# Keys and queries as half-precision pairs with a power of two per channel, the exponential undoing the power by its scale

## The chip, the cores and the metric

One Trainium2 chip; the kernel uses one of its cores. A core has TensorE (PE; its weight loader is listed apart as PEld), VectorE (DVE), ScalarE (ACT), GpSimd (POOL) and SyncE (SP), each taking its own instructions in order, and 16 DMA engines fed by queues. The metric is the device time of one execution in microseconds (us). A profiled execution gives a trace of every instruction.

## The reference

A trunk of two layers over 2048 tokens of width 1024: a Mamba-2 mixer, then multi-head latent attention (16 heads), then a final norm. The change touches the attention alone:

```python
ckv, k_rope = split(rms_norm(h, kv_g_in) @ kv_w_down)       # 256 and 32 columns
kv = rms_norm(ckv, kv_g_latent) @ kv_w_up                   # per head: k_nope 64, v 64
k_rope = rope(k_rope)
q  = rms_norm(cq, mla_g_q) @ mla_w_uq                       # per head: q_nope 64, q_rope 32
s  = (q_nope @ k_nope.T + q_rope @ k_rope.T) * 96 ** -0.5   # 96 channels
p  = softmax(where(causal, s, -inf))
o  = p @ v
```

The arithmetic is float32.

## The kernel before

Three stages follow each other: Mamba over four blocks of 512 tokens and four groups (16 items, each a scan of four chunks with the gemms of the next item between its steps), the projections of the attention (`mla`), and the attention itself (`heads`, about 2086 to 3010 us of the trace), then the output projection (`back`).

**A product of float32 accuracy** is three matmuls, `mm3` (lines 85 to 87): high part by high part, high by low, low by high. The parts come from `split` (lines 115, 116; with a scale of one value per channel 118, 119) as float32r pairs, or from `pair16` (lines 123, 124) as float16 pairs; in both ACT makes the high part and DVE the remainder. Already in half precision are most of Mamba's gemms, the values V and the probabilities. Keys and queries are float32r: `mla_up` writes them by `out` (channels without rotation) and `rope`, through POOL's DMA queue into `kn_d`, `qn_d`, `q1_d`, `q2_d`, `kr_d`, and `load_k`, `load_q` bring each head's back as tiles K (96 x 2 x 2048) and Q (96 x 2 x 512).

**The attention.** A head has four query blocks q of 512; each has four rows j of 128 queries, called q.j below. A row's keys up to the diagonal are cut into at most four pieces of 256 to 512 keys (3.1 has 3.1a to 3.1d; 40 pieces a head: 25 of 512 keys, 7 of 384, 8 of 256). The work on a piece and on its row:

- S: on PE, `mm3` of Q and K into one of four PSUM banks; the last piece of a row gets the mask by one more matmul (line 1062).
- M: on DVE, the maximum of the piece (line 1063). N: after the last piece, the row's negated maximum (line 1067).
- E: on ACT, the exponential of a piece, bias N, with its sum (line 1075; an ACTIVATE and a short ACTIVATION_READ_ACCUMULATOR). Only when it has ended is the piece's bank free: S of a piece waits for the E of the piece four before.
- T: a unit of 128 keys by up to four rows of probabilities is transposed on PE (line 1090, up to four transposes); P copies it to float16 on ACT (line 123), Q makes the low half on DVE (line 124), and V on PE multiplies it with the values (lines 1100, 1101). O, r and s are small steps at the end of a block or row.

PE's order here is written by hand: `CREDIT` says which T and V come after each piece, 20 pieces behind the scores. DVE, ACT and POOL take theirs from a scheduler when the program is built; the order is fixed from then on. Units are counted within a head, so T24, P24, Q24, V24 are one unit's steps.

PE's order, the same in every head (from row 2.0 on, cut):

```
S2.0c V10 V11 T15 V12 S2.1a T16 V13 S2.1b S2.1c V14 ... S2.3b S2.3c T24 V20 V21
S3.0a T25 S3.0b S3.0c S3.0d V22 V23 T26 T27 V24 T28 V25
S3.1a T29 S3.1b V26 S3.1c S3.1d V27 T30 T31 V28 T32 V29
S3.2a T33 S3.2b V30 S3.2c V31 S3.2d T34 V32 T35 T36 V33
S3.3a T37 V34 S3.3b V35 S3.3c S3.3d T38 V36 T39 V37 T40   S0.0a V38 T41 S0.1a (next head)
```

Of the kernel before, what the change touches and what calls it, by code (L numbers as in the profile page):

```python
# [9 lines left out]
F32 = mybir.dt.float32  # L10
# [10 lines left out]
P = 128  # L21
# [47 lines left out]
class Net:  # L69
# [205 lines left out]
    def constants(self, cp):  # L275
# [6 lines left out]
        for name, n in PACKED:  # L282
            setattr(self, name, self.pack[:, at:at + n])
            at += n

    def layer_constants(self, cp):
        nc, a = self.nc, self.a
# [41 lines left out]
    def mamba(self, cp):  # L329
# [45 lines left out]
        self.tail = self.outp(*items[-1])  # L375

    def value_scale(self):
# [29 lines left out]
        for k in range(2):  # L407
            nc.gpsimd.dma_start(self.wv_d[k * P:(k + 1) * P, :], raw[k])

    def load_x(self, b, src, tag="hx"):  # L410
# [404 lines left out]

    def rope(self, p1, p2, cos, sin, d1, d2, n, t0):
# [45 lines left out]
    def mla_kv_down(self, b, tables):  # L862
# [10 lines left out]
        for j in range(2):  # L873
# [3 lines left out]
            pk.append(ps)  # L877
        self.rope(pk[0], pk[1], *tables, self.kr_d[0:16], self.kr_d[16:32], 16, b * TB)

# [36 lines left out]
    def mla_up(self, b, tables):  # L916
# [11 lines left out]

        def out(ps, d):
# [15 lines left out]
        while ahead:  # L945
            (n, w), ahead = ahead, next(todo, None)
            qT = self.qT
            for i in range(2 if n == 6 else 4):
                r0 = n % 2 * 512 + i * P
                if n < 2:  # L950
                    out(chan(cT, w, i, "tr"), self.kn_d[r0:r0 + P])
                elif n < 4:
# [8 lines left out]
                elif n < 6:  # L961
                    out(chan(qT, w, i, "mm"), self.qn_d[r0:r0 + P])
                else:
                    self.rope(chan(qT, w, i, "mm"), chan(qT, w, i + 2, "mm"), *tables, self.q1_d[i * P:(i + 1) * P],
                              self.q2_d[i * P:(i + 1) * P], P, t0)
                yield
# [53 lines left out]
    def heads(self, sp):  # L1020
# [15 lines left out]
        def scores(h, qb, st):  # L1036
# [8 lines left out]
            for j in range(4):  # L1045
# [20 lines left out]
                nm = self.t(sp, "nm", [P, 1], bufs=4)  # L1066
                v.tensor_reduce(nm, mx[:, :nb], AX.X, ALU.max, negate=True)  # L1067
                p = {}
# [3 lines left out]
                def exp(n, j=j, nb=nb, parts=parts, banks=banks, nm=nm, p=p, sm=sm):  # L1072
                    s, w = banks[n]
                    x = self.t(sp, "Pr", [P, TB], bufs=NP)
                    nc.scalar.activation(x[:, :w], s[:, :w], AF.Exp, bias=nm, accum_out=sm[:, n:n + 1])  # L1075
                    for c in range(0, w, P):
# [195 lines left out]
    def run(self):  # L1272
        tc = self.tc
        with ExitStack() as whole:
# [8 lines left out]
            self.ri_d = dp.tile([NH, T], F32, name="ri_d")  # L1283
            self.qn_d = dp.tile([1024, 2, T], F32, name="qn_d")
            self.q1_d = dp.tile([256, 2, T], F32, name="q1_d")
            self.q2_d = dp.tile([256, 2, T], F32, name="q2_d")
            self.kn_d = dp.tile([1024, 2, T], F32, name="kn_d")
            self.kr_d = dp.tile([32, 2, T], F32, name="kr_d")
            self.v_d = dp.tile([T, 2048], F16, name="v_d")
# [60 lines left out]
```

## Time and profile before

| | us |
|---|---|
| median of 3 runs (3198.4 to 3201.17) | 3201.06 |
| the profiled execution | 3198.45 |
| its span, first to last instruction | 3196.7 |

The profile gives instructions with their line, engine, operation and tile (`mm<-K,xT` is a PSUM tile written from K and a Q tile, whose buffer is named xT), their start and duration, and the idle time of the engine before one with what ended it. Durations of neighbours overlap, since an engine starts an instruction before the one ahead has drained: what an instruction costs in a stream is the distance of two starts, what it costs in a chain is its duration. The start of a first matmul behind a weight load is modelled early; the starts of the second and third are not. A row "x4" in order of time merges equal neighbours: its duration reaches from the first start to the last end.

### The profile page before, as it was taken

How to read it: one execution, taken by the hardware profiler on the slowest of the kernel's cores; microseconds unless marked ns; L12 is line 12 of the kernel's file. 1: busy time of each engine (PE TensorE's matmuls, PEld its weight loads, DVE VectorE, ACT ScalarE, POOL GpSimd, SP SyncE). 2: the span in 40 equal slices, each digit the busy share in tenths (PEclk: the TensorE clock that was granted, in tenths of full speed). 3: DMA queues.
4: the chain of work that ended last, by engine and by line, in shares of the span. 5: the costliest groups of instructions: out<-in, count | busy, mean ns of one | idle time of the engine just before them, and what ended most of it. 6: DMA issues, size and time to landing. Idle time of an engine off the chain costs nothing.

```text
span 3196.7 us, 51296 instructions
## 1 busy us (share of the span) xinstructions
PE 3098.7 (97%) x17735; PEld 2244.6 (70%) x17735; DVE 2371.4 (74%) x4786; ACT 2016.2 (63%) x5027; POOL 658.8 (21%) x927
## 2 busy tenths in 40 slices
PE   8999999999999999999999999999999999999998
PEld 6787654556655566665878888877777777777777
DVE  6888787777666666766766665678888888888675
ACT  7888576665555464555646554477877778778522
POOL 1222232321122211312111211322222122222100
PEclk9999999999999999999999999999999999999999
DMA  5443656554343345534486655843434434444494
GB/s 176 131 128 125 225 190 230 189 183 154 133 166 125 120 143 185 172 120 138 128 273 222 222 191 192 266 111 77 92 79 85 86 77 92 81 97 104 99 274 158
DMA packets 213236, 482.52 MB, mean 151 GB/s; under 512 B 28976, under 2 KB 62768, under 8 KB 211536
## 3 DMA queue, kind: packets, MB, share of 16 engines
q1 hardware_dynamic: 160672, 316.02, 31.2%
q0 software_dynamic: 52304, 163.22, 18.9%
q8 instruction: 140, 2.29, 0.3%
q14 instruction: 120, 0.98, 0.1%
HBM read 347.02 MB, written 132.12 MB: 150 GB/s over the span
## 4 chain that ended last, share of the span: by engine, by line
PE 65%; DVE 8%; ACT 6%; DMA 5%; issue 2%; POOL 1%; SPq 0%; ACTq 0%; DVEq 0%; POOLq 0%
PE mm L85 13%; PE mm L86 12%; PE mm L87 12%; PE tr L1090 6%; PE tr L1100 3%; PE tr L1101 3%; PE tr L86 3%; PE tr L87 3%; PE tr L85 3%; DVE cacc L495 2%; DMA wraw<-in_ssm_w_in_dram 2%; PE tr L699 1%; ACT Pr L1075 1%; DMA os<-ri_d 1%; DMA big<-cumT 1%
## 5 line engine op out<-in xcount | busy, mean ns | idle before, releaser
L124 DVE SCALAR_TENSOR_TENSOR PTs<-tr,PTs 128x512 f16<-128x512 f32 (+3 forms) x640 | 375.0, 607 | 92.4 <-ACT PTs L123 86.6
L123 ACT ACTIVATE PTs<-tr 128x512 f16<-128x512 f32 (+3 forms) x640 | 328.5, 541 | 141.1 <-PE tr L1090 140.7
L1063 DVE TENSOR_REDUCE mx<-mm 128x1 f32<-128x512 f32 (+2 forms) x631 | 375.7, 608 | 46.8 <-PE mm L87 44.3
L1075 ACT ACTIVATE Pr<-mm,nm 128x512 f32<-128x512 f32 (+2 forms) x631 | 395.7, 636 | 23.1 <-DVE nm L1067 21.4
L1090 PE MATMUL tr<-pack,Pr 128*128 128x128 f32 x2176 | 317.6, 273 | 1.4 <-ACT Os L1107 1.3
L85 PE MATMUL mm<-xT,wsp 128*128 128x512 f16 (+1 forms) x800 | 310.3, 388 | 0.0
L85 PE MATMUL mm<-K,xT 96*128 96x512 f32 (+2 forms) x639 | 287.0, 449 | 23.3 <-ACT Pr L1075 21.9
L86 PE MATMUL mm<-xT,wsp 128*128 128x512 f16 (+1 forms) x800 | 307.6, 384 | 0.0
L87 PE MATMUL mm<-xT,wsp 128*128 128x512 f16 (+1 forms) x800 | 307.3, 385 | 0.2 <-DVE wsp L116 0.2
L1090 PEld LDWEIGHTS tr<-pack,Pr 128*128 128x128 f32 x2176 | 253.2, 141 | 49.8 <-ACT Os L1107 2.1
L495 DVE SCALAR_TENSOR_TENSOR cacc<-craw,pack,cacc 128x512 f32<-128x512 f32 x288 | 219.9, 785 | 27.6 <-ACT cacc L493 25.5
L85 PE MATMUL mm<-wsp,xT 128*128 128x512 f16 (+2 forms) x640 | 235.9, 369 | 3.1 <-ACT craw L489 3.0
L86 PE MATMUL mm<-wsp,xT 128*128 128x512 f16 (+2 forms) x640 | 234.2, 366 | 0.0
L87 PE MATMUL mm<-wsp,xT 128*128 128x512 f16 (+2 forms) x640 | 233.6, 366 | 0.0
L86 PE MATMUL mm<-K,xT 96*128 96x512 f32 (+2 forms) x639 | 231.8, 363 | 0.0
L87 PE MATMUL mm<-K,xT 96*128 96x512 f32 (+2 forms) x639 | 231.2, 362 | 0.0
L1100 PE MATMUL tr<-PTs,xT 128*128 128x512 f16 (+3 forms) x640 | 222.2, 349 | 0.1
L1101 PE MATMUL tr<-PTs,xT 128*128 128x512 f16 (+3 forms) x640 | 219.7, 347 | 0.0
L85 PE MATMUL mm<-wsp,yT 128*128 128x512 f32 x512 | 208.9, 408 | 8.4 <-DMA wsp<-wo_d 4.5
L692 ACT ACTIVATE Xw<-tr,d_wend 128x64 f32<-128x64 f32 x512 | 112.0, 329 | 155.8 <-DVE y L689 127.6
L86 PE MATMUL mm<-wsp,yT 128*128 128x512 f32 x512 | 204.1, 399 | 0.0
L87 PE MATMUL mm<-wsp,yT 128*128 128x512 f32 x512 | 203.9, 398 | 0.0
(421 smaller groups left out, 7417.9 us busy)
## 6 DMA issues: line engine op xcount, KB each, us to landing
wsp<-wo_d SPq DMA_DIRECT2D x96, 512.0 KB, 3.6
wraw<-in_ssm_w_in_dram SPq DMA_DIRECT2D x128, 256.0 KB, 3.0
big<-cumT SPq DMA_DIRECT2D x64, 512.0 KB, 4.7
wsp<-w_d SPq DMA_DIRECT2D x64, 512.0 KB, 3.7
wo_d<-wsp POOLq DMA_DIRECT2D x32, 512.0 KB, 4.6
w_d<-wsp POOLq DMA_DIRECT2D x32, 512.0 KB, 5.0
xT<-qn_d POOLq DMA_DIRECT2D x64, 256.0 KB, 4.6
K<-kn_d POOLq DMA_DIRECT2D x15, 1024.0 KB, 8.4
```

What stands on the lines that cost most here:

```text
L85: mm(out, l_hi, r_hi, start=start, stop=False)
L86: mm(out, l_hi, r_lo, start=False, stop=False)
L87: mm(out, l_lo, r_hi, start=False, stop=stop)
L123: self.nc.scalar.activation(hi, src, AF.Copy, scale=scale)
L124: self.nc.vector.scalar_tensor_tensor(lo, src, scale, hi, ALU.mult, ALU.subtract)
L495: nc.vector.scalar_tensor_tensor(acc, raw[:, k:k + TB], wk[k], acc, ALU.mult, ALU.add)
L692: act(Xw[:, hc], px[:, hc], AF.Copy, scale=wend[:, h0 + h:h0 + h + 1])
L1063: v.tensor_reduce(mx[:, n:n + 1], s[:, :w], AX.X, ALU.max)
L1075: nc.scalar.activation(x[:, :w], s[:, :w], AF.Exp, bias=nm, accum_out=sm[:, n:n + 1])
L1090: nc.tensor.transpose(pt[:, j * P:(j + 1) * P], st["P"][j][kb], self.ident)
L1100: nc.tensor.matmul(st["O"][:, c], vals[h][:, kb, :], u[:, 0], start=kb == 0, stop=False)
L1101: nc.tensor.matmul(st["O"][:, c], vals[h][:, kb, :], u[:, 1], start=False, stop=kb == nk - 1)
```

## The change

Keys and queries become float16 pairs. So that they fit float16, each channel is multiplied by a power of two; the product of the powers of a key channel and its query channel is the same number for all 96 channels of a head, and its inverse is given to the exponential as scale. In parts:

- New `qk_scale`, in the scan of Mamba's item (block 2, group 0), counted as 8 steps beside the item's 32. It bounds each channel by the sum of the weights' absolute values: 14 loads through the three buffers `wraw` (13 of 256 KB), 14 ACT instructions, 52 matmuls with 128 weight columns and 2 moving columns, 16 with 16 weight columns, 3 small ones, and about 25 DVE instructions on at most 24 columns. It fills `aK`, `bQ`, `aR`, `bR`, `sc`, `nsc`.
- In `mla_up` and `rope` the 88 pairs are made by `pair16` with a scale of one value per channel in place of `split` without one. Stores, DRAM tensors and loads have half the bytes; their number stays.
- A float32r matmul loads its weights itself; a float16 one has its own LDWEIGHTS instruction ahead of it (1920 more PE instructions). The wait for the bank is on the matmul, not on the load.
- N is one instruction that joins two maxima and multiplies by `nsc`, and rows of three or four pieces get one more ahead of it (t, 128 in all).
- E has two operands of one value per partition, bias and scale, where it had the bias alone.

PE's order in the attention is unchanged. The built program's orders on ACT and DVE are not; where they matter:

```
ACT  before  P13 P14 P15 E2.0a E2.0b P16 E2.0c
     after   P13 P14 P15 E2.0a P16 E2.0b E2.0c
DVE  before  Q13 Q14 M2.0b M2.0c N2.0 Q15 M2.1a
     after   M2.0b Q13 Q14 M2.0c t Q15 N2.0 M2.1a
DVE  before  M2.3b M2.3c s N2.3 Q24 M3.0a M3.0b s Q25 M3.0c M3.0d Q26 Q27 N3.0 Q28
     after   M2.3b M2.3c s Q24 t N2.3 M3.0a M3.0b M3.0c s Q25 M3.0d t N3.0 Q26 Q27 Q28
ACT  before  P24 E2.3a E2.3b E2.3c P25 O P26 P27 P28 E3.0a E3.0b E3.0c E3.0d P29 P30 P31 E3.1a
     after   P24 E2.3a E2.3b E2.3c P25 O P26 P27 E3.0a P28 E3.0b P29 E3.0c E3.0d P30 P31 E3.1a
ACT  before  E3.1d O P34 E3.2a P35 P36 E3.2b P37 E3.2c E3.2d P38 E3.3a P39 E3.3b P40 E3.3c
     after   E3.1d O P34 P35 P36 E3.2a E3.2b E3.2c P37 E3.2d P38 E3.3a P39 P40 E3.3b E3.3c
```

In Mamba the last chunk of the item's scan now stands among the small matmuls of `qk_scale`: between the item's last gemm and the next item's first, 16, 24, 6, 6 and 16 of them lie between the chunk's own matmuls.

```diff
+            elif g == 0 and b == NB - 2:
+                parts.append(self.qk_scale())
+                total += 8
...
+    def qk_scale(self):
...
+        for u in range(5):
+            ks = 2 if u < 2 else 3
+            src, gain = (a["kv_w_up"], self.gkl) if u < 2 else (a["mla_w_uq"], self.gqs)
+            c0 = u * TB if u < 2 else (u - 2) * TB
+            w = []
+            for k in range(ks):
+                raw = self.t(self.wp, "wraw", [P, TB], bufs=WRAW)
+                nc.sync.dma_start(raw, src[k * P:(k + 1) * P, c0:c0 + TB])
+                if k % 2 == 0:
+                    m = self.t(self.wp, "wsp", [P, 2, TB], F32R, bufs=WSP)
+                nc.scalar.activation(m[:, k % 2], raw, AF.Abs, scale=gain[:, k:k + 1])
+                w.append(m[:, k % 2])
+            yield
+            ps = self.t(self.pp, "tr", [P, TB], bufs=4)
+            for c in range(4):
+                for k in range(ks):
+                    nc.tensor.matmul(ps[:, 2 * c:2 * c + 2], w[k][:, c * P:(c + 1) * P], self.ones_r[:, 0:2],
+                                     start=k == 0, stop=k == ks - 1)
...
-            u = self.ev()
-            self.split(u[:n, 0, :], u[:n, 1, :], x[:n])
-            nc.gpsimd.dma_start(d[:, :, t0:t0 + TB], u[:n].bitcast(F32))
+            u = self.ev(F16)
+            self.pair16(u[:n, 0, :], u[:n, 1, :], x[:n], scale[:n])
+            nc.gpsimd.dma_start(d[:, :, t0:t0 + TB], u[:n])
...
-            u = self.ev()
-            self.split(u[:, 0, :], u[:, 1, :], ps)
-            nc.gpsimd.dma_start(d[:, :, t0:t0 + TB], u.bitcast(F32))
+            u = self.ev(F16)
+            self.pair16(u[:, 0, :], u[:, 1, :], ps, scale)
+            nc.gpsimd.dma_start(d[:, :, t0:t0 + TB], u)
...
-            self.keys[h] = self.t(self.hp, "K", [96, 2, T], F32R, bufs=2)
+            self.keys[h] = self.t(self.hp, "K", [96, 2, T], F16, bufs=2)
...
-        Q = self.quer[h, n] = self.t(self.xq, "xT", [96, 2, TB], F32R, bufs=8)
+        Q = self.quer[h, n] = self.t(self.xq, "xT", [96, 2, TB], F16, bufs=8)
...
-                v.tensor_reduce(nm, mx[:, :nb], AX.X, ALU.max, negate=True)
+                if nb == 1:
+                    v.tensor_scalar(nm, mx[:, 0:1], self.nsc, None, ALU.mult)
+                else:
+                    if nb > 2:
+                        v.tensor_tensor(mx[:, 0:nb - 2], mx[:, 0:nb - 2], mx[:, 2:nb], ALU.max)
+                    v.scalar_tensor_tensor(nm, mx[:, 0:1], mx[:, 1:2], self.nsc, ALU.max, ALU.mult)
...
-                    nc.scalar.activation(x[:, :w], s[:, :w], AF.Exp, bias=nm, accum_out=sm[:, n:n + 1])
+                    nc.scalar.activation(x[:, :w], s[:, :w], AF.Exp, bias=nm, scale=self.sc, accum_out=sm[:, n:n + 1])
```

More of the change, by code (lines that the diff above doesn't have):

```diff
@@ L408, in value_scale @@
             nc.gpsimd.dma_start(self.wv_d[k * P:(k + 1) * P, :], raw[k])
+    def qk_scale(self):
+        nc, v, a = self.nc, self.nc.vector, self.a
+        S = self.t(self.sm, "qkS", [P, 24], bufs=1)
+        v.memset(S, 1.0)
+        for u in range(5):
[16 more added lines that the diff above has]
+                                     start=k == 0, stop=k == ks - 1)
+            v.tensor_copy(S[:, 4 * u:4 * u + 4], ps[:, 0:8].rearrange("p (c n) -> p c n", n=2)[:, :, 0])
+        raw = self.t(self.wp, "wraw", [P, KD, 32], bufs=WRAW)
+        nc.sync.dma_start(raw, a["kv_w_down"][:, 256:288].rearrange("(k p) c -> p k c", p=P))
+        v.tensor_tensor(raw, raw, self.gk.unsqueeze(2).to_broadcast([P, KD, 32]), ALU.mult)
+        m = self.t(self.wp, "wsp", [P, KD, 32], F32R, bufs=WSP)
+        nc.scalar.activation(m, raw, AF.Abs)
+        yield
+        ps = self.t(self.pp, "tr", [P, TB], bufs=4)
+        for k in range(KD):
+            for i in range(2):
+                nc.tensor.matmul(ps[0:16, 0:2], m[:, k, 16 * i:16 * i + 16], self.ones_r[:, 0:2],
+                                 start=k + i == 0, stop=k + i == KD)
+        v.tensor_copy(S[0:16, 20:21], ps[0:16, 0:1])
+        sel = self.t(self.sp, "cacc", [16, P], bufs=2)
+        v.tensor_copy(sel.rearrange("p (n i) -> p n i", n=8), self.ident[0:16, 0:16].unsqueeze(1).to_broadcast([16, 8, 16]))
+        ps = self.t(self.pp, "tr", [P, TB], bufs=4)
+        nc.tensor.matmul(ps[:, 0:1], sel, S[0:16, 20:21], start=True, stop=True)
+        v.tensor_copy(S[:, 20:21], ps[:, 0:1])
+        v.tensor_tensor(S[:, 16:18], S[:, 16:18], S[:, 18:20], ALU.add)
+        v.tensor_scalar(S, S, TINY, None, ALU.max)
+        ei = self.t(self.sm, "qke", [P, 24], I32, bufs=1)
+        v.tensor_scalar(ei, S.bitcast(I32), 23, None, ALU.logical_shift_right)
+        e = self.t(self.sm, "qkf", [P, 24], bufs=1)
+        v.tensor_copy(e, ei)
+        t = self.t(self.sm, "qkt", [P, 16], bufs=1)
+        v.tensor_tensor(t[:, 0:8], e[:, 0:8], e[:, 8:16], ALU.add)
+        v.tensor_scalar(t[:, 8:10], e[:, 16:18], e[:, 20:21], 1.0, ALU.add, ALU.add)
+        v.tensor_reduce(t[:, 10:11], t[:, 0:10], AX.X, ALU.max)
+        yield
+        ps = self.t(self.pp, "tr", [P, TB], bufs=4)
+        nc.tensor.transpose(ps[0:1, 0:P], t[:, 10:11], self.ident)
+        v.tensor_reduce(t[0:1, 11:12], ps[0:1, 0:P], AX.X, ALU.max)
+        ps = self.t(self.pp, "tr", [P, TB], bufs=4)
+        nc.tensor.matmul(ps[:, 0:1], self.ones[0:1, :], t[0:1, 11:12], start=True, stop=True)
+        v.tensor_scalar(t[:, 12:13], ps[:, 0:1], 193.0, None, ALU.max)
+        x = self.t(self.sm, "qkx", [P, 20], bufs=1)
+        v.tensor_scalar(x[:, 0:8], e[:, 0:8], -1.0, 264.0, ALU.mult, ALU.add)
+        v.tensor_scalar(x[:, 8:16], e[:, 0:8], t[:, 12:13], 263.0, ALU.subtract, ALU.add)
+        v.tensor_scalar(x[:, 16:17], e[:, 20:21], -1.0, 263.0, ALU.mult, ALU.add)
+        v.tensor_scalar(x[:, 17:18], e[:, 20:21], t[:, 12:13], 264.0, ALU.subtract, ALU.add)
+        v.tensor_scalar(x[:, 18:19], t[:, 12:13], -146.0, None, ALU.add)
+        v.tensor_scalar(x[:, 0:19], x[:, 0:19], 1.0, 254.0, ALU.max, ALU.min)
+        xi = self.t(self.sm, "qki", [P, 20], I32, bufs=1)
+        v.tensor_copy(xi[:, 0:19], x[:, 0:19])
+        v.tensor_scalar(xi[:, 0:19], xi[:, 0:19], 23, None, ALU.logical_shift_left)
+        f = xi.bitcast(F32)
+        v.tensor_copy(self.aK, f[:, 0:8])
+        v.tensor_copy(self.bQ, f[:, 8:16])
+        v.tensor_copy(self.aR, f[:, 16:17])
+        v.tensor_copy(self.bR, f[:, 17:18].to_broadcast([P, 2]))
+        v.tensor_copy(self.sc, f[:, 18:19])
+        v.tensor_scalar(self.nsc, f[:, 18:19], -1.0, None, ALU.mult)
+        yield
@@ L814, in rope_tables, with rope @@
         return cos, ang
-    def rope(self, p1, p2, cos, sin, d1, d2, n, t0):
+    def rope(self, p1, p2, cos, sin, d1, d2, n, t0, scale):
         nc, v = self.nc, self.nc.vector
@@ L927, in chan, with out @@
             return ps
-        def out(ps, d):
-            u = self.ev()
-            self.split(u[:, 0, :], u[:, 1, :], ps)
-            nc.gpsimd.dma_start(d[:, :, t0:t0 + TB], u.bitcast(F32))
+        def out(ps, d, scale):
+            u = self.ev(F16)
+            self.pair16(u[:, 0, :], u[:, 1, :], ps, scale)
+            nc.gpsimd.dma_start(d[:, :, t0:t0 + TB], u)
         def groups():
@@ L950, in mla_up @@
                 if n < 2:
-                    out(chan(cT, w, i, "tr"), self.kn_d[r0:r0 + P])
+                    out(chan(cT, w, i, "tr"), self.kn_d[r0:r0 + P], self.aK[:, 4 * n + i:4 * n + i + 1])
                 elif n < 4:
@@ L961, in mla_up @@
                 elif n < 6:
[L962 removed]
+                    c = 4 * (n - 4) + i
+                    out(chan(qT, w, i, "mm"), self.qn_d[r0:r0 + P], self.bQ[:, c:c + 1])
                 else:
                     self.rope(chan(qT, w, i, "mm"), chan(qT, w, i + 2, "mm"), *tables, self.q1_d[i * P:(i + 1) * P],
[L965 removed]
+                              self.q2_d[i * P:(i + 1) * P], P, t0, self.bR[:, i:i + 1])
                 yield
```

15 lines of the change are left out of this document (9 added, 6 removed).

## The prediction

> **What bounds the kernel now.** I read the page's head and its busy times first, then the busy times of three windows (the columns are the window, its length, then the busy time and instructions of PE, PEld, DVE, ACT and POOL, the granted clock, the DMA share and GB/s).
>
> ```profile
> span 3196.7 us, 51296 instructions
> PE 3098.7 (97%) x17735; PEld 2244.6 (70%) x17735; DVE 2371.4 (74%) x4786; ACT 2016.2 (63%) x5027; POOL 658.8 (21%) x927
> ...
> 840.00:945.00 105.00, 104.63 (x601) 63.17 (x601) 67.02 (x121) 53.78 (x135) 20.22 (x27) 1.00 0.46 161
> 1800.00:2000.00 200.00, 197.83 (x1027) 170.48 (x1026) 122.09 (x242) 104.63 (x203) 33.73 (x55) 1.00 0.61 201
> 2086.00:3010.00 924.00, 899.27 (x5655) 687.53 (x5654) 772.07 (x1831) 733.72 (x2010) 201.55 (x295) 1.00 0.41 84
> ```
>
> PE sets the pace in all three: the scan where `qk_scale` goes (840 to 945), the projections whose pairs change (1800 to 2000) and the attention (2086 to 3010). In the attention ACT (733.72 of 924) and DVE (772.07) are not far behind; that window alone has matmuls to save. What holds PE up there is told by the group of the first score matmul on the page, and by the view of who waits for the exponential.
>
> ```profile
> L85 PE MATMUL mm<-K,xT 96*128 96x512 f32 (+2 forms) x639 | 287.0, 449 | 23.3 <-ACT Pr L1075 21.9
> ...
>   PEld mm L85: 57.3, 118
>   PE mm L85: 21.9, 21
> ```
>
> PE loses only some 23 us, all at S, all to E: the bank comes free late. Both sides of the change meet here: shorter S, and a longer E that comes at another place of ACT's order.
>
> **Faster score matmuls.** The spacing of starts is the price. Here are a float32r S of 256 keys, one of 384, and a stretch that holds float16 V of 384 columns, then an S of 512.
>
> ```profile
> 2496.33 0.28 PE L86 MATMUL mm<-K,xT 96*128 96x256 f32 x1
> 2496.45 0.28 PE L87 MATMUL mm<-K,xT 96*128 96x256 f32 x1
> ...
> 2521.41 0.34 PE L86 MATMUL mm<-K,xT 96*128 96x384 f32 x1
> 2521.59 0.34 PE L87 MATMUL mm<-K,xT 96*128 96x384 f32 x1
> ...
> 2517.60 0.33 PE L1100 MATMUL tr<-PTs,xT 128*128 128x384 f16 x1
> 2517.77 0.33 PE L1101 MATMUL tr<-PTs,xT 128*128 128x384 f16 x1
> ...
> 2518.49 0.39 PE L86 MATMUL mm<-K,xT 96*128 96x512 f32 x1
> ```
>
> And the stretch in which S3.1a waits today:
>
> ```profile
> 2509.01 1.04 PE L1090 MATMUL tr<-pack,Pr 128*128 128x128 f32 x8
> ...
> 2510.33 0.60 PE L1090 MATMUL tr<-pack,Pr 128*128 128x128 f32 x4
> 2510.76 0.38 PE L1100 MATMUL tr<-PTs,xT 128*128 128x512 f16 x1
> 2510.98 0.38 PE L1101 MATMUL tr<-PTs,xT 128*128 128x512 f16 x1
> 2512.57 0.50 PE L85 MATMUL mm<-K,xT 96*128 96x512 f32 x1 [1.21 <-ACT Pr L1075]
> 2512.90 0.39 PE L86 MATMUL mm<-K,xT 96*128 96x512 f32 x1
> 2513.13 0.40 PE L87 MATMUL mm<-K,xT 96*128 96x512 f32 x1
> ```
>
> A float32r matmul of 512 costs .23 (2512.90 to 2513.13; .233 over several), a float16 one .216 (2510.76 to 2510.98); at 384 it is .18 against .17 (.163 by columns), at 256 .12 against .11. For three matmuls that is .05, .05 and .03 saved. A head has 25, 7 and 8 such pieces: 25 x .05 + 7 x .05 + 8 x .03 = 1.84 us, and 16 heads give **-29 us**, if no wait eats it. The 1920 separate weight loads cost nothing as long as a matmul of .11 or more covers them.
>
> **The longer exponential.** No row has an ACTIVATE with a scale and a bias of one value per partition. The nearest are pairs of groups with none and with one such operand, first from SBUF, then from PSUM:
>
> ```profile
> L115 ACT ACTIVATE wsp<-wraw 128x512 fp32r<-128x512 f32 x132 | 82.9, 629 | 42.9 <-DMA wraw<-in_kv_w_up_dram 13.3 <-PE tr L87 8.3 <-PE mm L87 5.6
> L118 ACT ACTIVATE wsp<-wraw,pack 128x512 fp32r<-128x512 f32 x40 | 28.7, 727 | 25.4 <-DMA wraw<-in_ssm_w_out_dram 17.4 <-PE mm L87 7.8
> L123 ACT ACTIVATE PTs<-tr 128x512 f16<-128x512 f32 x448 | 258.5, 600 | 88.0 <-PE tr L1090 87.5
> L489 ACT ACTIVATE craw<-mm,un 128x512 f32<-128x512 f32 x72 | 48.5, 674 | 3.1 <-PE mm L87 3.0
> ```
>
> The first operand adds .10 and .07. The second is unseen: 0 to .10; I take .09, since nothing says that it is free. E then takes .78 instead of the .69 below, and follows another E at .76 instead of .67. That alone is 640 x .09 = 58 us of ACT, which has 190 us idle in the attention; it counts only where a wait ends on E.
>
> **Where waits end.** In order of time, ACT and DVE at the wait of S3.1a:
>
> ```profile
> 2509.72 1.08 ACT L123 ACTIVATE PTs<-tr 128x512 f16<-128x512 f32 x2
> 2511.02 0.60 ACT L123 ACTIVATE PTs<-tr 128x512 f16<-128x512 f32 x1 [0.22 <-PE tr L1090]
> 2511.74 0.69 ACT L1075 ACTIVATE Pr<-mm,nm 128x512 f32<-128x512 f32 x1
> 2512.32 0.19 ACT L1075 ACTIVATION_READ_ACCUMULATOR Pr<-mm,nm 128x1 f32 x1
> 2512.41 0.68 ACT L1075 ACTIVATE Pr<-mm,nm 128x512 f32<-128x512 f32 x1
> ...
> 2510.35 1.29 DVE L124 SCALAR_TENSOR_TENSOR PTs<-tr,PTs 128x512 f16<-128x512 f32 x2 [0.26 <-ACT PTs L123]
> 2511.55 0.15 DVE L1067 TENSOR_REDUCE nm<-mx 128x1 f32<-128x4 f32 x1
> 2511.65 0.69 DVE L124 SCALAR_TENSOR_TENSOR PTs<-tr,PTs 128x512 f16<-128x512 f32 x1
> ```
>
> From these come the links. T of four is .44 on PE (1.04 less a single .27, over seven: .11 each). From the end of T's slot to P is .25 (2510.33 + .44 to 2511.02). P to the next is .48 (1.08 less .60), to its own end .60; Q starts .03 later, takes .60 (1.29 less .69). N is .15 and reaches E .04 later: .20 as a link; t I price like it, .19. From E's end to S is .24 today (2512.43 to the slot that ends at 2512.90, so 2512.67); with the weights already loaded I take .10, between 0 and .24. V of 512 is .43, S of 512 after the change .65. Today's stall at S3.1a is 2512.67 less 2511.20 (2510.98 + .22): 1.47. At S3.2a it is 2518.49 - .23 less 2517.77 + .17: .32. At S3.3a it is nothing:
>
> ```profile
> 2523.80 0.38 PE L1101 MATMUL tr<-PTs,xT 128*128 128x512 f16 x1
> ...
> 2524.25 0.40 PE L86 MATMUL mm<-K,xT 96*128 96x512 f32 x1
> ```
>
> (2523.80 + .22 = 2524.25 - .23.) Now each wait after the change, by the orders shown above: the chain that frees the bank, against PE's own work meanwhile.
>
> - S2.1b waits for E2.0a. N2.0 now stands behind Q15, so from T15: .44 + .25 + P15 .60 + .03 + Q15 .60 + N .20 + E .78 + .10 = 3.00. PE has T15, V12, S2.1a, T16, V13: .44 + .43 + .65 + .44 + .43 = 2.39. Stall .61. S2.1c waits for E2.0b, now behind P16: .76 + .48 + .78 + .10 = 2.12 against .78 + .10 + S2.1b .65 = 1.53: .59. Together 1.20.
> - S3.0b waits for E2.3a, with N2.3 behind Q24 and t: 3.00 + .19 = 3.19. PE has T24, V20, V21 (384), S3.0a, T25: .44 + .43 + .33 + .65 + .44 = 2.29. Stall .90. S3.0c and S3.0d follow with nothing between, an E of .76 for an S of .65: .11 each. Together 1.12.
> - S3.1a waits for E3.0a, now one P earlier: V22 .22, V23 .11, T26 and T27 .87, then .25 + P27 .48 + E .78 + .10 = 2.81 against 1.20 + V24 .43 + T28 .44 + V25 .43 = 2.50. Stall .31, where it is 1.47 today. S3.1b and S3.1c each find one P ahead of their E: 2.12 against .88 + .65 + .43, .16 each; S3.1d .11. Together .74.
> - S3.2a: its chain is not reordered; I leave .32. S3.2b and S3.2c with a P between, .16 each. Together .64.
> - S3.3a waits for E3.2a, now behind P35 and P36: T34 .44, V32 .43, T35 and T36 .88, then .25 + .48 + .78 + .10 = 3.36, against the same 1.75 and V33 .43 = 2.18. Stall 1.18.
> - S0.1a waits for E3.3b, now behind P40: T40 .44 + .25 + .48 + .78 + .10 = 2.05, against T40 .44, S0.0a with its mask .45, V38 .43, T41 .33 = 1.65. Stall .40.
>
> The sum is 5.28 a head, against 1.47 + .32 = 1.79 today: +3.49, times 16 **+56 us**. With the row-first stalls alone (.61 + .90 + .31 + .32 + 1.18 = 3.32) it is +24; with .24 in place of .10 at the seven large ones (+1.0) +72. A late S delays its M and T, which I do not count again: ACT and DVE are idle while PE waits.
>
> **`qk_scale`.** Its matmuls stand in a stretch where PE is busy 104.63 of 105 us, so they add. The float32r loads and the loads it makes have these rows:
>
> ```profile
> L86 PEld LDWEIGHTS mm<-K,xT 96*128 96x128 f32 x631 | 120.4, 191 | 8.2
> L1101 PEld LDWEIGHTS <-xT 128*128 128x128 f16 x640 | 62.8, 98 | 14.8 <-issue 0.2
> ...
> wraw<-in_kv_w_up_dram SPq DMA_DIRECT2D x16, 256.0 KB, 3.0
> ```
>
> With two moving columns the weights set the price: .11 (a T) to .19 each, so 52 cost 5.7 to 9.9; the 16 of 16 columns at most .11, 0 to 1.8. I take 8. The last chunk of the scan and a load late in the queue can leave PE empty for 0 to 10; I take 4. **+12 us**, 6 to 22. SP's queue gets 14 loads ahead of those of the next output gemm; at 3.0 us each through three buffers they fit in the 105 us unless a buffer is held.
>
> **The projections.** 88 ACT instructions get .10 longer; PE is busy 197.83 of 200 us there and ACT 104.63, DVE 122.09, which hides it: 0, and 9 us if the four banks come free late. Half the bytes: PE waits for no K or Q load, so 0, at most a gain of 2 where the attention starts.
>
> **Sum**: 3198.45 - 29 + 56 + 12 = 3237. The profiled execution is 2.6 us under the median shown. Its own bounds: -29 + 24 + 6 - 2 gives 3197, -29 + 72 + 22 + 9 gives 3272.
>
> **The rivals.**
> - R1, faster: stalls are exchanged, not added. S3.1a gives back what S3.3a opens, and a stall early in a block lets ACT and DVE catch up, so that the next does not come; ACT's 58 us fall into its 190 us idle. Then 3198.45 - 29 + 12 = 3181. For it: ACT waits for PE at L123 88 us long. Against it: the chains above start at different T's, each after the last stall has ended. It decides if a head stalls under 1.79 + 17 / 16 = 2.9 us. Chance .17.
> - R2: the orders bite, but the second operand is free. Twelve links lose .09: 4.2 a head, +2.4, +38; 3219. For it only that its price is unseen. Chance .12.
> - R3: `qk_scale` stands in PE's way: loads wait for a `wraw` buffer, PE in its strict order for them. 14 loads at 3.0 are 42 us, half of it shown: +20, 3257. Against it: 105 us to hide them. Chance .08.
> - R4: float16 at 96 rows runs at float32r's pace (the float16 rows here have 128): 3237 + 29 = 3266. Chance .04.
> - R5: weight loads, .19 against .10, set PE's pace: 3 x 631 x .093 = 176 us less, 3198.45 - 176 + 56 + 12 = 3090. Against it: matmuls of 256 keys follow each other at .12 although each load is recorded at .19. Chance .02. (The Trainium skill, "Perfetto Trace Analysis", section "Identifying the Most-Contended Engine", holds matmul busy time a bad measure and would judge by the busy share of LDWEIGHTS, 70% here; by that rule R5 would be a gain to look for, but the .12 spacing disagrees.)
>
> **How the numbers follow.** The forecast has .57. Its own range is 3197 to 3272. To 3188 R2 and a part of R1 come in; R4 lies within 3268, R5 and most of R1 stay out: 3188 to 3268. A measurement of this kernel tells about 0.2% (6.4 us) from no change. Faster by more: R1, R5 and a little of R2, .20; within: the low ends of the forecast and R2, .06; slower .74.
>
> **What would show it.** In the profile after: starts of L86 and L87 at .216 for 512 keys (R4: .233); E near .78 (R2: .69); PE's idle time before S of 3.3a about 1.2, of 3.0b .9, of 2.1b .6, of 3.1a fallen to .3 (R1: their sum under 2.9 a head); the window of Mamba's item about 12 longer, not 30 (R3). I am wrong if the sum of stalls in a head stays near today's, or if a late S shifts ACT's whole work and opens stalls in blocks that I called free.

## The result and the profile after

| | us |
|---|---|
| changed kernel, median of 4 runs (3249.98 to 3251.65) | 3250.71 |
| kernel before beside it, median of 4 runs | 3201.11 |
| ratio, 95% interval | 1.0156 (1.0143 to 1.0168) |
| span of the profiled execution, before and after | 3196.7 and 3249.0 |

The change costs 1.6%; 3237 was predicted, in a range of 3188 to 3268. The page of the changed kernel begins so:

```profile
span 3249.0 us, 51511 instructions
## 1 busy us (share of the span) xinstructions
PE 3102.9 (96%) x17808; PEld 2141.7 (66%) x17808; DVE 2415.6 (74%) x4947; ACT 2087.3 (64%) x5041; POOL 660.6 (20%) x927
```

The span is cut in three by the first start and the last end of an exponential: the attention starts at 2086.8 before and 2095.5 after (+8.7), lasts 906.8 and 952.1 us (+45.3), and what follows it takes 203.1 and 201.4 (-1.7). The sum is the 52.3 us between the spans. So nearly all of the loss lies in the attention, where the matmuls got shorter. Its window, moved by the later start (same columns as in the prediction):

```profile
2096.00:3020.00 924.00, 855.04 (x5383) 542.58 (x5382) 773.52 (x1889) 753.66 (x1931) 189.37 (x281) 0.99 0.26 57
```

Before, PE was busy 899.27 of 924 us there; now 855.04, and it gets through 5383 matmuls in place of 5655. PE idles, although neither ACT (753.66) nor DVE (773.52) is full. The groups of the page for E and for S's first matmul, then two groups of N and t from the view by form, then from the view of who waits for E:

```profile
L1174 ACT ACTIVATE Pr<-mm,nm,sc 128x512 f32<-128x512 f32 (+2 forms) x631 | 452.0, 727 | 52.7 <-DVE nm L1166 46.0
...
L85 PE MATMUL mm<-K,xT 96*128 96x512 f16 (+2 forms) x639 | 224.0, 350 | 68.6 <-ACT Pr L1174 65.0
```

```profile
L1166 DVE SCALAR_TENSOR_TENSOR nm<-mx,nsc 128x1 f32<-128x1 f32 x192 | 44.9, 234 | 3.9
L1165 DVE TENSOR_TENSOR mx<-mx 128x2 f32<-128x2 f32 x64 | 12.1, 189 | 2.2
```

```profile
who waited for it (us, times):
  POOL o_d L1212: 68.5, 11
  PE mm L85: 65.0, 113
```

(The means of N and t hold three slow instructions, which the experiments come back to; the medians are 219 and 161 ns.) PE's idle time ahead of S has gone from 23.3 to 68.6 us, nearly all of it on E. And a second row has changed: ACT now idles 52.7 us ahead of E, 46.0 of them until N. The wait is a chain over three engines, last maximum, N, E, S, and every link of it got longer or later. Here is S3.0b in one head, PE first, then ACT, then DVE:

```profile
2532.35 0.38 PE L85 MATMUL mm<-K,xT 96*128 96x512 f16 x1
2532.57 0.38 PE L86 MATMUL mm<-K,xT 96*128 96x512 f16 x1
2532.78 0.38 PE L87 MATMUL mm<-K,xT 96*128 96x512 f16 x1
2533.00 0.60 PE L1189 MATMUL tr<-pack,Pr 128*128 128x128 f32 x4
2534.45 0.38 PE L85 MATMUL mm<-K,xT 96*128 96x512 f16 x1 [0.85 <-ACT Pr L1174]
```

```profile
2531.87 0.58 ACT L123 ACTIVATE PTs<-tr 128x512 f16<-128x512 f32 x1
2533.53 0.78 ACT L1174 ACTIVATE Pr<-mm,nm,sc 128x512 f32<-128x512 f32 x1 [1.08 <-DVE nm L1166]
2534.20 0.19 ACT L1174 ACTIVATION_READ_ACCUMULATOR Pr<-mm,nm,sc 128x1 f32 x1
2534.30 0.77 ACT L1174 ACTIVATE Pr<-mm,nm,sc 128x512 f32<-128x512 f32 x1
```

```profile
2532.48 0.69 DVE L124 SCALAR_TENSOR_TENSOR PTs<-tr,PTs 128x512 f16<-128x512 f32 x1
2533.09 0.15 DVE L1165 TENSOR_TENSOR mx<-mx 128x1 f32<-128x1 f32 x1
2533.27 0.22 DVE L1166 SCALAR_TENSOR_TENSOR nm<-mx,nsc 128x1 f32<-128x1 f32 x1
```

Read it backwards: S3.0b starts .14 after E has ended (2533.53 + .78); E began when N was done; N stands behind t and Q24 on DVE, Q24 behind P24 on ACT, P24 behind T24. ACT did nothing for 1.08 us and PE nothing for 1.01 (T's slot ends at 2533.00 + .44). The three S matmuls at the top also show the gain: starts .215 apart.

S3.3a shows the other half of the forecast, E3.2a behind P35 and P36:

```profile
2550.55 0.38 PE L1200 MATMUL tr<-PTs,xT 128*128 128x512 f16 x1
2551.99 0.38 PE L85 MATMUL mm<-K,xT 96*128 96x512 f16 x1 [1.06 <-ACT Pr L1174]
```

```profile
2550.10 1.09 ACT L123 ACTIVATE PTs<-tr 128x512 f16<-128x512 f32 x2 [0.21 <-PE tr L1189]
2551.07 0.78 ACT L1174 ACTIVATE Pr<-mm,nm,sc 128x512 f32<-128x512 f32 x1
```

2551.99 - (2550.55 + .22) = 1.22 us, at a place that had no wait before.

For `qk_scale` the view of its line of 128-column weights has:

```profile
L442 PEld LDWEIGHTS tr<-ones,wsp x52: 188/192/338, 937.4 to 946.3; 128*128 128x128 f32 x52
L442 PE MATMUL tr<-ones,wsp x52: 165/250/352, 937.5 to 946.4; 128*128 128x2 f32 x52
```

All 52 start within 8.9 us, with matmuls of the scan's last chunk among them.

### The profile page after: what moved, and what is told of

The parts are those of the page before. It is cut to its first block, busy times and chain, and to the rows that moved or that the text cites. A ratio compares the mean times of both kernels' runs of the same rounds, so it can differ in the third digit from the quotient of the medians.

```text
span 3249.0 us, 51511 instructions
## 1 busy us (share of the span) xinstructions
PE 3102.9 (96%) x17808; PEld 2141.7 (66%) x17808; DVE 2415.6 (74%) x4947; ACT 2087.3 (64%) x5041; POOL 660.6 (20%) x927
## 4 chain that ended last, share of the span: by engine, by line
PE 34%; ACT 11%; DVE 8%; issue 4%; DMA 2%; POOL 0%; ACTq 0%; SPq 0%; DVEq 0%; POOLq 0%
PE mm L85 6%; PE mm L87 6%; PE mm L86 6%; ACT Pr L1174 6%; PE tr L87 3%; PE tr L85 3%; PE tr L86 3%; ACT PTs L123 3%; DVE PTs L124 3%; PE tr L1189 2%; DVE mx L1157 2%; PE tr L1199 1%; PE tr L1200 1%; ACT Os L1206 1%; DVE nm L1166 0%
## 5 line engine op out<-in xcount | busy, mean ns | idle before, releaser
L1174 ACT ACTIVATE Pr<-mm,nm,sc 128x512 f32<-128x512 f32 (+2 forms) x631 | 452.0, 727 | 52.7 <-DVE nm L1166 46.0
L85 PE MATMUL mm<-K,xT 96*128 96x512 f16 (+2 forms) x639 | 224.0, 350 | 68.6 <-ACT Pr L1174 65.0
L86 PEld LDWEIGHTS <-xT 96*128 96x128 f16 (+1 forms) x1024 | 100.1, 98 | 198.4 <-issue 122.8
L87 PE MATMUL mm<-K,xT 96*128 96x512 f16 (+2 forms) x639 | 223.7, 350 | 0.0
L86 PE MATMUL mm<-K,xT 96*128 96x512 f16 (+2 forms) x639 | 223.3, 349 | 0.0
L85 PE MATMUL mm<-wsp,yT 128*128 128x512 f32 x512 | 209.2, 409 | 6.7 <-DVE sz L618 3.2
L86 PE MATMUL mm<-wsp,yT 128*128 128x512 f32 x512 | 204.8, 400 | 0.0
```

The costliest lines, as they stand in the source:

```text
L85: mm(out, l_hi, r_hi, start=start, stop=False)
L86: mm(out, l_hi, r_lo, start=False, stop=False)
L87: mm(out, l_lo, r_hi, start=False, stop=stop)
L1174: nc.scalar.activation(x[:, :w], s[:, :w], AF.Exp, bias=nm, scale=self.sc, accum_out=sm[:, n:n + 1])
```

## The experiments

Two measures serve throughout beside the ratio. The stall at a piece is the distance of the ends of S's first matmul and of the matmul ahead of it, less what it is where nothing waits (.216, .163, .110 us for float16; .235, .176, .118 for float32r), as a mean over the second to fifteenth head; a head's sum takes those above .03. The attention is the stretch from the first exponential to the last. Where the order of ACT and DVE matters, a third measure is given: the length of a head, from the first S of one head to the first S of the next, as a mean over heads 2 to 14. The experiments came in three groups, each beside its own runs of the kernel before (medians 3203.92, 3204.85, 3200.75), so ratios are compared, and a difference of ratios is turned into us by 3200.

| run | median us | ratio to before (95%) | stalls, us a head | attention, us |
|---|---|---|---|---|
| before | | 1 | 1.91 | 906.8 |
| changed kernel | 3250.71 | 1.0156 (1.0143 to 1.0168) | 6.31 | 952.1 |
| no_qk_scale | 3240.2 | 1.0113 (1.0098 to 1.0129) | 6.36 | 952.7 |
| no_qk_scale_old_order | 3231.37 | 1.0086 (1.0069 to 1.0103) | 5.73 | 945.8 |
| f16_new_order | 3203.64 | 0.9998 (0.9988 to 1.0007) | 4.26 | 910.7 |
| f16_alone | 3165.75 | 0.9877 (0.9862 to 0.9892) | 1.89 | 874.2 |
| operand_alone | 3203.95 | 1.0000 (0.9991 to 1.0010) | 4.02 | 918.9 |
| new_n_alone | 3196.64 | 0.9972 (0.9961 to 0.9983) | 3.48 | 909.2 |
| f32_both | 3264.6 | 1.0182 (1.0167 to 1.0197) | 5.20 | 966.8 |
| powers_of_product_one | 3174.88 | 0.9908 (0.9892 to 0.9925) | 1.92 | 874.5 |
| product_one_e30_first | 3162.38 | 0.9880 (0.9864 to 0.9897) | 1.14 | 864.2 |
| f16_e30_first | 3155.14 | 0.9856 (0.9842 to 0.9871) | 1.15 | 864.7 |

**Without `qk_scale`.** The attention stays as it is in the changed kernel.

```diff
-            elif g == 0 and b == NB - 2:
-                parts.append(self.qk_scale())
-                total += 8
+        for one in (self.aK, self.bQ, self.aR, self.bR, self.sc):
+            nc.vector.memset(one, 1.0)
+        nc.vector.memset(self.nsc, -1.0)
```

> The changed kernel without qk_scale: the six scale tiles are filled with 1 (nsc with -1), so the powers are left out and every instruction of the attention stays as in the changed kernel, in the same order on each engine. The trace of the changed kernel begins its attention 8.7 us later than before, so by that reading this run takes 3250.7 - 8.7 = 3242 us. If qk_scale costs nothing that the scan does not hide, it stays at 3251; if its matmuls are dearer than they look there (the 12 us of the prediction), 3239.

Measured: 3240.2, the attention as long as ever (952.7), its start at 2084.2 in place of 2095.5. `qk_scale` costs 11.3 us by the start of the attention and 14 by the ratios (1.0156 - 1.0113); the later pair powers_of_product_one and f16_alone gives 7.6 and 10. The sharpest measure is the stretch of Mamba in which it stands (about 890 to 1150 us, cut at the same matmuls in every trace): 261.6 to 262.4 us in the nine traces without it, 271.1 to 272.8 in the three with it. So it costs 9 to 11 us, and the rest of the loss is in the attention.

**Order or operand?** The changed kernel differs in the attention by three things besides float16: the scale operand, the new N, and the order of ACT and DVE that the scheduler made of them. To hold the order fixed, each instruction of ACT and DVE in heads 2 to 15 got an edge to its forerunner, which orders them on their engine and adds no wait:

```diff
+        for order in (ACT_ORDER, DVE_ORDER):
+            last = None
+            for h in range(1, NH - 1):
+                for w in order.split():
...
+                    if ins is not None:
+                        if last is not None:
+                            self.tc.add_manual_dep(ins, last.name, info, reason="order")
+                        last = ins
```

The two lists are the orders of one head read from the kernel before ("old") and from the changed kernel ("new"). The first and the last head keep what the scheduler makes of them, and in the kernel before the fifteenth has an order of its own (E3.0a ahead of P28), which the old list overrules. So it is heads 2 to 14 that have the order named. First operand and new N in the old order:

> As no_qk_scale, but ACT and DVE take their instructions of the attention in the order of the kernel before (t right ahead of N); the exponential keeps its scale operand, N its new form. Order theory: most of the loss is the order; the stalls fall from 6.3 us a head to about 3.0 (3.1a 1.8, 3.2a 0.5, and 0.1 at each of some six S that follow an E of 0.76 with an S of 0.65), against 1.9 before, while S and its mask save 1.9: 3201 - 0.8 x 16 = 3188 us. Operand theory: the longer E causes the loss in whatever order, so it stays near 3242.

Then the other corner: float16 alone, no operand and the old N, in the new order. Against the kernel before:

```diff
-            self.split(u[:, 0, :], u[:, 1, :], ps)
+            self.pair16(u[:, 0, :], u[:, 1, :], ps)
...
-            self.keys[h] = self.t(self.hp, "K", [96, 2, T], F32R, bufs=2)
+            self.keys[h] = self.t(self.hp, "K", [96, 2, T], F16, bufs=2)
...
```

> The kernel before with float16 pairs alone: no powers, no scale operand at the exponential, N as before; but ACT and DVE take their instructions of the attention in the order of the changed kernel. Order theory: the chains are only 0.09 shorter for each E in them, about 5.1 us of stalls a head: 3201 + (5.1 - 1.9 - 1.9) x 16 = 3222 us. Operand theory: the stalls go away with the operand, 3201 - 1.9 x 16 = 3171.

And the corner with neither, the order left to the scheduler:

> The kernel before with float16 pairs alone: no powers, no scale operand, N as before, and the scheduler's own order, which comes out as before but for N3.0, one Q later. Both theories: the saving of the shorter S comes whole, 3201 - 1.9 x 16 = 3171 us. If shorter S only lengthens the wait for E that follows (a bound by ACT), it stays within 5 us of 3201.

The four corners as ratios:

| | old order | new order |
|---|---|---|
| neither operand nor new N | 0.9877 | 0.9998 |
| both | 1.0086 | 1.0113 |

Both theories miss a part. The order alone costs .0121, 39 us: 4.26 us of stalls a head, at the places that were worked out for it (2.1b .55, 2.1c .40, 3.0b .66, 3.3a 1.13, 0.1a .35). The order theory had 5.1 a head there and 3222 us; it is too high by 18. But operand and N cost .0209, 67 us, in the old order too, and once they are there the new order adds only .0027, 9 us. (The intervals of those two runs overlap, so the traces have to bear this out: heads 2 to 14 last 55.06 us with neither, 57.61 with the order alone, 59.27 with operand and N, 59.69 with all. Over sixteen heads that is 41, 67 and 74 us, and 7 from the third to the last.) The order theory's 3188 us for that run is wrong by 43; what the operand theory said (near 3242) is nearer. Putting the old order back would not have rescued the change. This is what the old order looks like with them, at S2.2b, which never waits in the kernel before; PE, then ACT, then DVE:

```profile
2505.16 0.38 PE L1129 MATMUL tr<-PTs,xT 128*128 128x512 f16 x1
2505.95 0.38 PE L98 MATMUL mm<-K,xT 96*128 96x512 f16 x1 [0.41 <-ACT Pr L1101]
```

```profile
2505.03 0.78 ACT L1101 ACTIVATE Pr<-mm,nm,sc 128x512 f32<-128x512 f32 x1 [0.47 <-DVE nm L1093]
2505.70 0.19 ACT L1101 ACTIVATION_READ_ACCUMULATOR Pr<-mm,nm,sc 128x1 f32 x1
2505.80 0.77 ACT L1101 ACTIVATE Pr<-mm,nm,sc 128x512 f32<-128x512 f32 x1
```

```profile
2504.13 0.42 DVE L1084 TENSOR_REDUCE mx<-mm 128x1 f32<-128x256 f32 x1
2504.58 0.16 DVE L1092 TENSOR_TENSOR mx<-mx 128x1 f32<-128x1 f32 x1
2504.77 0.22 DVE L1093 SCALAR_TENSOR_TENSOR nm<-mx,nsc 128x1 f32<-128x1 f32 x1
2504.91 0.88 DVE L1121 SCALAR_TENSOR_TENSOR PTs<-tr,PTs 128x384 f16<-128x384 f32 x2
```

No P and no Q stands in this chain. From the end of the row's last maximum (2504.55) to the start of E are .48 us, where one N of .15 and a gap of .04 stood, and E is .78 in place of .69. That is .38 more in the chain, and PE waits .57.

f16_alone, whose order comes out as before (but for some places on DVE in the first head), shows that the gain of the change is real: its stalls are those of before (1.89 against 1.91), and the attention is 32.6 us shorter. It came out below the 3171 us expected, because the projections got some 5 us shorter as well (see the projections below).

**Operand and N apart**, both in the old order:

```diff
-                    nc.scalar.activation(x[:, :w], s[:, :w], AF.Exp, bias=nm, accum_out=sm[:, n:n + 1])
+                    nc.scalar.activation(x[:, :w], s[:, :w], AF.Exp, bias=nm, scale=self.sc, accum_out=sm[:, n:n + 1])
```

> f16_alone (3165.75 us, 1.9 us of stalls a head) with the scale operand at the exponential (a tile of ones) and nothing else: N as one reduction, the order of the kernel before. The run with operand and new N in that order has 5.7 us of stalls a head. Its stalls at 3.0c, 3.0d, 3.2b, 3.2d, 3.3b, 3.3c (1.1 us together, E pitch against S) should be the operand's, those at first and second pieces of rows 0.2, 1.3, 2.1, 2.2, 3.0 and the growth at 3.1a (2.5 us) belong to a chain with N and E in it. Operand theory: E at 0.09 more, 40 times a head, brings nearly all of it: stalls over 4.5 a head, 3208 us or more. N theory: the longer link from the last maximum to E, 0.25 to 0.3 where E has 0.09, brings the larger part: stalls about 3.6 a head, 3192 us.

```diff
-                v.tensor_reduce(nm, mx[:, :nb], AX.X, ALU.max, negate=True)
+                if nb == 1:
+                    v.tensor_scalar(nm, mx[:, 0:1], self.nsc, None, ALU.mult)
+                else:
+                    if nb > 2:
+                        v.tensor_tensor(mx[:, 0:nb - 2], mx[:, 0:nb - 2], mx[:, 2:nb], ALU.max)
+                    v.scalar_tensor_tensor(nm, mx[:, 0:1], mx[:, 1:2], self.nsc, ALU.max, ALU.mult)
```

> f16_alone with the new N alone (t and a maximum times nsc, nsc a tile of -1), the exponential without a scale operand, in the order of the kernel before. Operand theory: N costs little, stalls under 2.6 a head, under 3177 us. N theory: stalls about 3.7 a head, 3195 us. If the two costs only bite together, neither this run nor operand_alone reaches half of the 66 us between f16_alone and the run with both.

Measured against f16_alone: the operand .0123, 39 us, 4.02 us of stalls; the new N .0095, 30 us, 3.48. Their sum is .0218 against .0209 together: they add. The operand fell between its two expectations, above what the N theory left for it; the N came out as the N theory said (3196.64 for 3195). Each of them spoils 1.6 to 2.1 us a head. Where shows the kind. With the operand small stalls appear all over (0.2a .19, 1.3a .16, 2.1b .20, 2.2b .31, 3.0b .15, 3.0d .28, 3.2d .17, 3.3c .17); with the new N they sit at few places that wait for a row's first exponentials (2.2b .38, 3.1a 1.83 for 1.32, 3.3a .22; without the fifteenth head 3.1a is 1.63 for 1.36). Their groups, E in operand_alone and N in new_n_alone:

```profile
L1095 ACT ACTIVATE Pr<-mm,nm,sc 128x512 f32<-128x512 f32 x395 | 308.3, 787 | 28.4 <-DVE nm L1087 26.5
```

```profile
L1093 DVE SCALAR_TENSOR_TENSOR nm<-mx,nsc 128x1 f32<-128x1 f32 x192 | 43.6, 227 | 5.2
```

The 227 holds one N of 2.35 us. In the fifteenth head POOL splits weights of the output projection (TENSOR_TENSOR on W, 2.34 us each). A t, or an N that joins two maxima, that starts while one of these runs ends .02 us after it, in all five traces that have the new N: in the changed kernel an N takes 1.64 us (at 2932.09), a t 1.99 (2963.05) and the N behind it 2.26 (2965.07), beside POOL instructions that start at 2931.36, 2962.67 and 2964.98. The old N, a TENSOR_REDUCE, takes .11 to .16 beside them. In that head S3.1a waits 4.45 us in new_n_alone, and S3.2a 4.16 in the changed kernel. This is a second price of the new N, paid in one head.

In heads 2 to 14 a head is 2.49 us longer with the operand, 1.42 with N and 4.21 with both, over sixteen heads 40, 23 and 67 us. So some 7 of N's 30 us come on top in the other three heads, and the rest holds where the order is that of before.

**Is the shorter S to blame as well?** Operand and N on the float32r kernel, in the order of before:

```diff
+        nc.vector.memset(self.sc, 1.0)
+        nc.vector.memset(self.nsc, -1.0)
...
-                    nc.scalar.activation(x[:, :w], s[:, :w], AF.Exp, bias=nm, accum_out=sm[:, n:n + 1])
+                    nc.scalar.activation(x[:, :w], s[:, :w], AF.Exp, bias=nm, scale=self.sc, accum_out=sm[:, n:n + 1])
```

(N as in the diff before.)

> The kernel before with its float32r keys and queries, the scale operand (ones) at the exponential and the new N, in the order of the kernel before. If operand and N alone are the cause, the loss is as with float16: 3201 + 66 = 3267 us. If the shorter S (less cover) is part of it, a float32r piece covers 0.05 more for each S in a chain and 0.05 of each E pitch, some 15 to 25 us of the loss: about 3245 us.

Measured +.0182, 58 us, against 67 with float16; stalls grow by 3.29 a head against 3.84. The missing cover is about 9 us by both (the intervals of the ratios leave 0 to 17) and 12 by the length of heads 2 to 14 (3.44 us more against 4.21), less than the 15 to 25 that were given for it; most of the loss is there without a single float16 score. At 3.0b, 2.1b and 3.1a the two runs are within .11 of each other. The differences lie at 1.3a (.04 for .25) and 2.2b (.44 for .57) and at the small stalls between neighbours (3.0c .06 for .11, 3.2d .05 for .16), where an E of .76 meets an S of .65 or of .70; 0.0a goes the other way (.23 for .12).

**A version that keeps the powers.** If the power of a query channel is the inverse of that of its key channel, the exponential needs no scale and N no factor. Against the changed kernel, beside the two lines that go back to the old E and N:

```diff
-        v.tensor_scalar(t[:, 12:13], ps[:, 0:1], 193.0, None, ALU.max)
+        v.tensor_scalar(t[:, 12:13], ps[:, 0:1], 0.0, 273.0, ALU.mult, ALU.add)
...
-        v.tensor_scalar(x[:, 0:8], e[:, 0:8], -1.0, 264.0, ALU.mult, ALU.add)
-        v.tensor_scalar(x[:, 8:16], e[:, 0:8], t[:, 12:13], 263.0, ALU.subtract, ALU.add)
+        v.tensor_scalar(x[:, 0:8], e[:, 0:8], -1.0, 258.0, ALU.mult, ALU.add)
+        v.tensor_scalar(x[:, 8:16], e[:, 0:8], t[:, 12:13], 269.0, ALU.subtract, ALU.add)
...
```

> The changed kernel with qk_scale and its powers, but with the power of a query channel the inverse of its key channel's, so that the product is 1: the exponential has no scale operand and N is the one reduction of before. The scheduler then gives the order of before. Expected from f16_alone plus the price of qk_scale (10 us between the changed kernel and no_qk_scale): 3176 us, faster than both kernels. If the scale of one value per channel at the 88 pairs costs time after all, it is more.

Measured 3174.88, ratio 0.9908: the attention of f16_alone (874.5 us) and `qk_scale` ahead of it. The scale per channel at the 88 pairs is hidden, as predicted (the projections below). The scheduler, left alone, gives the order of before. The price is range: the query's own bound no longer enters, so a query channel whose values exceed float16 after the key's inverse power would overflow; f16_alone, with no powers, needs keys and queries to fit float16 as they are. No run tried either limit.

**The order, once E is short.** Two moves that the new order had among others, put into the old one:

```diff
-    "P35- E12 E13 P36- E14 P37- P38- E15 E16 P39- E17 P0 P1 E18 E19 P2 P3 O3- E20 P4 E21 E22 E23 P5 O0 P6 P7 P8 E24 "
+    "P35- E12 E13 P36- E14 P37- P38- E15 E16 P39- E17 P0 P1 E18 E19 P2 P3 O3- E20 P4 E21 E22 E23 P5 O0 P6 P7 E24 P8 "
...
-    "M18 Q39- M19 s9 M20 N10 Q0 Q1 M21 Q2 Q3 M22 M23 s10 N11 Q4 M24 M25 s11 Q5 M26 M27 Q6 Q7 N12 Q8 M28 s12 M29 Q9 "
+    "M18 Q39- M19 s9 M20 N10 Q0 Q1 M21 Q2 Q3 M22 M23 s10 N11 Q4 M24 M25 s11 Q5 M26 M27 N12 Q6 Q7 Q8 M28 s12 M29 Q9 "
```

(E24 is E3.0a, N12 is N3.0, M27 is M3.0d; P and Q are counted here from 0 at the head's own first unit, 20 below the numbers used so far; a minus sign marks the head before.)

> powers_of_product_one (3174.88 us) with two places of the order moved, all else as before: N3.0 right behind M3.0d instead of behind two Q, and E3.0a ahead of the P that stands before it. S3.1a stalls 1.32 us a head there and 0.35 in f16_new_order, where both moves are made among others; S3.1b may take back 0.2 to 0.3. If the order is worth something of itself once E is short, the gain is about 0.7 x 16 = 11 us: 3164 us. If the stall only moves on to 3.1b, 3.1c and 3.2a, it stays at 3172 to 3178.

> f16_alone (3165.75 us) with the same two moves: by the same reckoning 3155 us, or 3163 to 3169 if the stall moves on.

Measured 3162.38 and 3155.14, near the 3164 and 3155 of a real gain. By ratio the gains are 9 and 7 us, and the intervals of each pair just overlap; the traces decide: heads 2 to 14 are .87 and .81 us shorter. S3.1a falls from 1.32 to .35, S3.1b takes .18, and no other piece changes by more than .03. In f16_e30_first, after V and with its E already under way:

```profile
2486.72 0.38 PE L1115 MATMUL tr<-PTs,xT 128*128 128x512 f16 x1
2487.26 0.38 PE L97 MATMUL mm<-K,xT 96*128 96x512 f16 x1 [0.17 <-ACT Pr L1087]
```

Both versions beat the kernel before and the changed one.

## Why the prediction was right, point by point

**Faster matmuls, -29.** Right: spacing .215 to .216 at 512, and f16_alone's attention is 32.6 us shorter with stalls as before. The few us above the sum are the mask matmul behind a float16 S, which takes .058 in place of .073 (16 a head, 4 us in all); at 384 keys the spacings are .176 and .163, a saving of .04 and not .05, 1 us less. R4 is out. R5 is out too: PEld's busy time fell by 103 us (2244.6 to 2141.7), and the run got longer.

**The longer exponential.** Right: .787 for .695 at 512 keys, and the same .09 at 384 (.670 for .582) and 256 (.592 for .498); it is a price of each instruction, not of its width. R2 put it at nothing: out. Its 4.2 us a head of stalls were nearly met where the operand is indeed absent (f16_new_order, 4.26).

**The waits, +56.** The mechanism and the places were right, the sum too small; measured are 6.31 - 1.91 = 4.40 more a head, 70 us over sixteen, where 3.49 were forecast. By piece:

| | predicted | measured | | predicted | measured |
|---|---|---|---|---|---|
| 2.1b | .61 | .73 | 3.1a | .31 | .44 |
| 2.1c | .59 | .49 | 3.1b to 3.1d | .43 | .37 |
| 3.0b | .90 | 1.03 | 3.2a | .32 | .59 |
| 3.0c, 3.0d | .22 | .38 | 3.2b to 3.2d | .32 | .31 |
| 0.1a | .40 | .53 | 3.3a | 1.18 | 1.22 |
| 0.0a, 2.2c | 0 | .21 | | | |

The terms mis-sized are two links. From E's end to S I took .10; the median of the 148 waits over .2 us is .143. N I priced by the old reduction, .15 and .04 to E; the median of the new instruction is .22. The two, .11 together, are what 2.1b and 3.0b are short by in most heads (.10 and .11 by their medians). S3.2a was left as it was, and is .32 in thirteen heads; its mean of .59 is the fifteenth head alone, where t and N end only with POOL's instruction. Two small stalls (0.0a, 2.2c) were not seen.

A sum over all sixteen heads closes the account of the attention. The waits at S grow from 37.2 to 104.4 us, 67 more. Waits at the other matmuls, for which the forecast had no term, grow from 2.9 to 11.3 (what the distance of two ends lies above the median of the same pair of instructions). The shorter S and mask give back 32. That makes 43 of the 45.3 us.

**What the account of the waits got wrong** is whose loss it is. Of its 56 us it let the new order carry most (R2, order without operand, had 38) and the operand the rest, and N hardly anything. The mechanism of the sum holds for the order that was built. But the runs show that the order isn't what must be undone: in the old order operand and N still cost 67 of the 76 us that lie between f16_alone and the run with all three (1.0113 - 0.9877), 39 and 30 each by itself (N's 30 with the fifteenth head's share). The chain last maximum, N, E, S had just enough cover in the kernel before. Lengthened, it ends late in whichever order; the scheduler's order only chose other places for the wait. Why the 39 us that the new order costs alone shrink to 9 beside the others was not tried further; that both lengthen the same chains, whose stalls do not add, fits the tables but is argued.

**R1**, stalls exchanged one for one, asked for a sum under 2.9 a head: it is 6.31. S3.1a did fall, by .99, as R1 and the forecast both had it; S3.3a alone took back more. That ACT idles 52.7 us ahead of E, waiting for N, shows why its 190 idle us didn't absorb the longer E: they don't lie where the chain runs.

**`qk_scale`, +12.** Right: 9 to 11 us where it stands. R3's 30 is out.

**The projections, 0.** Half right. The longer ACT instructions are hidden: the last 1800 matmuls ahead of the first S take 366.4 us in f16_alone and as much in powers_of_product_one, which has the scale per channel. But the stretch itself got shorter, which the forecast put at 0: 371.3 us before and 371.8 in f32_both, 364.5 to 366.5 in the ten traces with float16 pairs, 366.2 in the changed kernel. PE's waits there (3.3 us before) are gone in the changed kernel, and the DMA moves 171 GB/s in place of 215. Whether the halved bytes or the other instructions bring these 5 us was not tried.

**The total** came nearer than its terms, which is in part luck. The waits cost 75 us (67 and 8) where 56 were forecast; S gave back 32 for 29, `qk_scale` cost about 10 for 12, and the projections gained 5 that were not forecast. That is +48 where +39 was forecast; the medians differ by 49.6.

## What to carry to other kernels

Here an operand of a tenth of a microsecond cost nothing at the pairs of the projections, where the engine has time to spare, and 39 us in a chain that hands buffers back and is walked a dozen times a head; in the same chain, .29 us more between a row's last maximum and E cost 30. Price a change by the chain that it lengthens and the cover of that chain, not by the engine's idle time. When a scheduler reacts to a change, measure the change in the old order and the new order without the change before blaming either. And a scaling that has to be undone at run time belongs where it cancels (here in the inverse power on the other factor), not in the hot loop.

## What the runs showed of the hardware

The second operand of one value per partition costs ACT .09 us for each ACTIVATE at 512, 384 and 256 columns (787, 670 and 592 ns after, 695, 582 and 498 before); for the first, the prediction's two pairs of rows have .10 and .07.

On DVE two maxima of one column, joined and multiplied by such an operand, take .22 us, and the t ahead of them .16, against .14 to .16 for a reduction of one to four columns. Such a t or N that starts while POOL's TENSOR_TENSOR on W runs ends with it, after up to 2.35 us; TENSOR_REDUCE, and TENSOR_SCALAR with .20 to .21, are not held up beside the same instruction.

A float16 S that waits for its bank starts .14 us after ACT has ended. With float32r the slot begins .24 after it (the median of 40 waits; 2512.43 to 2512.67 in the prediction's rows). There the wait sits on the weight load: in the kernel before PEld waits for E 118 times, 57.3 us, and in the changed kernel's view of who waits for E PEld doesn't appear. The load that needn't wait saves .10 at every such wait.
